# Which matmuls of a seven-product step run ahead of the next step's first: a change of order on TensorE

## The chip, the cores and the metric

One core of one Trainium2 chip. The metric is the device time of one execution in microseconds (us): the median of three runs before the change, and the same for the changed kernel. A profile is one execution of its own, with its own time. The engines are called as the profile calls them: PE (TensorE's matmuls), PEld (TensorE's weight loads), DVE (VectorE), ACT (ScalarE), POOL (GpSimd), SP (SyncE).

## What is computed

A decoder trunk of two layers on 256 positions of width 2048, all in float32. What matters here are its five matrix products per layer, the last above all:

```python
for l in range(DEPTH):                      # 2 layers
    h = rms_norm(x, norm1_g[l])
    z = h @ w_in[l]                         # 2048 x 5120
    ...                                     # attention and gated groups give mix
    x = x + mix @ w_out[l]                  # 2048 x 2048
    h2 = rms_norm(x, norm2_g[l])
    x = x + jnp.square(jax.nn.relu(h2 @ w_up[l])) @ w_down[l]   # 2048 x 8192, 8192 x 2048
return rms_norm(x, final_g)
```

## The kernel before

**Numbers.** Every weight and every activation is split in two parts, a rounded high part and the low rest. A product of two such numbers is made of three matmuls: high by high, low by high, high by low. The weights come from memory in blocks of 128 x 1024 (`Sub`), which SP's queue loads into one of 7 raw buffers; ACT makes the high part (`high`, line 167) and DVE the low part (`low`, line 177). There are 6 buffers each for high and for low parts.

**Steps.** The work of TensorE is a list of steps in a fixed order, and everything else hangs on it. Before a step is issued, the high and low parts of some sub-blocks ahead are issued (lines 1004 and following), and delayed work (`soon`, `later`) whose time has come. Time is counted in sub-blocks done. There are three kinds of steps that carry weights:

- Channel-major steps (`transposed`, matmuls at lines 400, 402 and 404): one sub-block, two blocks of 128 output channels (`cb`) by four blocks of rows (`k`) by three matmuls, 24 in all. The weights stand in the array, 256 positions of the activation stream through it. The first matmul of a step needs its high part, the second (line 402) its low part.
- Position-major steps (`natural`, lines 459 to 461), 12 matmuls of 512 columns. They do not stand near the change.
- Seven-product steps (`fast`, matmuls at lines 430, 432 and 433), for a part of the columns of `w_down`. They make a 2 x 2 block product from seven products instead of eight, by sums and differences of blocks (Winograd's form of Strassen's scheme). Here the activations stand in the array and 256 columns of weights stream. One step has four sub-blocks: two that are loaded (`Top`, `Bottom`) and two made of sums (`Sums`), for which DVE runs four subtractions (lines 218, 219, 222 and 223). The sub-blocks are used in the order top, bottom, first sums (`upper`), second sums (`lower`). Each of the seven products is two blocks `k` by three matmuls, so a step has 42.

**Where a seven-product step ends.** Six of the products, 36 matmuls, are issued in the step. The seventh, which uses `lower` as the sixth does, is put into the list `left_over`, and the next channel-major step issues its 6 matmuls behind its own first three (line 395). Each seven-product step is followed by a channel-major step.

**Where the results go.** Two steps (`p` 0 and 1) make one group. The first six results of a group lie in halves of three banks of the accumulator memory, the seventh in a half of a bank of its own. When the group's second step is done, ACT copies the three banks (line 901) for groups 1 and 2, and the seventh half five sub-blocks later (line 887; for group 0 line 869). GpSimd adds the copies up in memory over the eight row blocks of `w_down` (line 866).

**Where the steps stand.** In each layer the up and down projections run in nine rounds `e`. Round `e` makes 1024 hidden channels from `w_up` and uses those of round `e - 1` with `w_down`. `ORDER` and `USUAL` give the place of each seven-product step among the channel-major ones, for instance ahead of steps 2 and 3, 7 and 9, 13 and 14. At the end of the up projection of a round DVE has more to do: it makes low parts of the new hidden channels (line 643) and sums of them (lines 796 to 799), and the seven-product steps that follow need those.

Of the kernel before, what the change touches and what calls it, by code (L numbers as in the profile page):

```python
# [35 lines left out]
P = 128  # L36
# [29 lines left out]
USUAL = ((7, 9), (2, 3), (13, 14))  # L66
WARM = 11
HALVES = 5
D_SCORES, D_NORM, D_TURN, D_VALUES = 2, 1, 3, 2


# [19 lines left out]
def trunk(ctx: ExitStack, tc: tile.TileContext, layout, xT, consts, gains, w, b_sp, w_sp, out):  # L91
# [11 lines left out]
    vec, act, pe = nc.vector, nc.scalar, nc.tensor  # L103
# [30 lines left out]
    def acc_bank(i=None, of=4):  # L134

        if i is None:
            i = bank_at[0] = (bank_at[0] + 1) % of
        return pacc.tile([P, 512], F32, name=f"acc{i}", tag=f"acc{i}")
# [61 lines left out]
    class Bottom(Sub):  # L200


        left, right, frees = Top.left, Top.right, 0
# [46 lines left out]
    def run_due(calls=due):  # L250
        for item in [i for i in calls if i[0] <= now[0]]:
            calls.remove(item)
            item[1]()
# [102 lines left out]
    left_over = []  # L356
    summed, sum_parts = [True], [None]

    def sums_ready():
        run_until(lambda: summed[0])  # L360
# [8 lines left out]
    def transposed(name, l, row0, nk, col0, ncols, moving, after, between=None, apart=False, of=4, cols=None):  # L369

        cols = cols or range(0, ncols, 256)
        order = [(c, k) for c in cols for k in range(0, nk, 4)]
        if between:
            h = nk // 8
            order[h:2 * h], order[2 * h:3 * h] = order[2 * h:3 * h], order[h:2 * h]  # L380
        accs = {}
        for n, (c, k0) in enumerate(order):
            if between and n == nk // 4:
                mark(between)
            wt = Sub(name, l, row0 + k0 * P, col0 + c, 4, 256)

            def mm(wt=wt, k0=k0, c=c):
                two = apart and c == cols[-1]
                if k0 == 0:
                    accs[c] = [acc_bank(of=of), acc_bank(of=of)] if two else acc_bank(of=of)  # L390
                ps = accs[c]
                for cb in range(2):
                    o = ps[cb][:, 0:S] if two else ps[:, cb * S:(cb + 1) * S]
                    for k in range(4):
                        if cb == 0 and k == 1 and left_over:
                            left_over.pop()()
                        xs = moving(k0 + k)
                        hi = wt.hi[:, k, cb * P:(cb + 1) * P]
                        last = k0 + k == nk - 1
                        pe.matmul(o, lhsT=hi, rhs=xs[:, 0, :], start=(k0 + k == 0 and (two or cb == 0)), stop=False,  # L400
                                  skip_group_check=True)
                        pe.matmul(o, lhsT=wt.lo[:, k, cb * P:(cb + 1) * P], rhs=xs[:, 0, :], start=False, stop=False,  # L402
                                  skip_group_check=True)
                        pe.matmul(o, lhsT=hi, rhs=xs[:, 1, :], start=False, stop=last, skip_group_check=True)  # L404
            steps.append((wt, mm, (lambda c=c: after(c, accs[c])) if k0 + 4 == nk else None))

    def fast(name, l, row0, col0, tiles, slots, fresh, last, done):

        o = []
        for p in range(2):
            top, bottom = (cls(name, l, row0 + (4 * h + 2 * p) * P, col0, 2, 512) for h, cls in enumerate((Top, Bottom)))
            upper, lower = Sums(top, bottom, False), Sums(top, bottom, True)

            def mm(p=p, top=top, bottom=bottom, upper=upper, lower=lower):
                if p == 0:
                    o.extend(slots())  # L420
                half = tiles[0][0]
                sums_ready()
                extra = sum_parts[0]
                left, right = slice(0, 256), slice(256, 512)

                def product(n, a, lower_rows, tt, b, cols):
                    for k in range(2):
                        xh, xl = (a[:, 4 * lower_rows + 2 * p + k, i, tt * P:(tt + 1) * P] for i in range(2))
                        hi, lo = b.hi[:, k, cols], b.lo[:, k, cols]
                        pe.matmul(o[n], lhsT=xh, rhs=hi, start=(p == 0 and k == 0 and n in fresh), stop=False,  # L430
                                  skip_group_check=True)
                        pe.matmul(o[n], lhsT=xh, rhs=lo, start=False, stop=False, skip_group_check=True)  # L432
                        pe.matmul(o[n], lhsT=xl, rhs=hi, start=False, stop=(n in last and p == 1 and k == 1),  # L433
                                  skip_group_check=True)

                for n, args in enumerate((
                        (half, 0, 0, top, left), (half, 1, 0, bottom, left), (extra, 1, 0, bottom, right),
                        (extra, 1, 1, upper, left), (extra, 0, 1, upper, right), (extra, 0, 0, lower, right))):
                    product(n, *args)
                left_over.append(lambda: product(6, half, 1, 1, lower, left))  # L440
            steps.append(((top, bottom, upper, lower), mm, (lambda: done(o)) if p and done else None))

    def natural(name, l, col0, ncols, after):
# [20 lines left out]
    def mark(fn):  # L464

        steps.append((None, fn, None))
# [484 lines left out]
    def load_more():  # L951
        while n_load[0] < len(subs):
# [6 lines left out]
            if 0 < c < KC:  # L959
                nc.sync.dma_start(x[:, c:c + 2, :], xv[:, c:c + 2, :])  # L960
            subs[n_load[0]].load(2 if n_load[0] < HALVES else 1)
            n_load[0] += 1
            n_raw[0] += 1

    def high_to(n, parts=1):
        while n_high[0] < min(n, len(subs)):
            if not subs[n_high[0]].loads:
                low_to(n_high[0] - subs[n_high[0]].second)
            subs[n_high[0]].high(parts)
            n_high[0] += 1  # L970

    def low_to(n, parts=1):
        while n_low[0] < min(n, len(subs)):
            subs[n_low[0]].low(parts)
            n_raw[0] -= subs[n_low[0]].frees
            n_low[0] += 1
# [22 lines left out]
    for n, (wt, mm, after) in enumerate(steps):  # L999
# [3 lines left out]
        else:  # L1003
            ahead = min(2 + max(done - 10, 0) // 2, LO_BUFS - 2)
            if done + 2 < KC // 2:
                norms[0].chunks(2 * done + 4)
            high_to(min(done + 2 + ahead, HALVES), 2)
            high_to(done + 2 + ahead)
            run_due()
            low_to(min(done + 1 + ahead, HALVES), 2)  # L1010
            low_to(done + 1 + ahead)
# [12 lines left out]
    n = norms[-1]  # L1024
# [43 lines left out]
```

## Time and profile before

| What | Value |
|---|---|
| Median of 3 runs | 2031.38 us (2031.15 to 2032.34) |
| Profiled execution, its own time | 2032.32 us |
| Its span, first to last instruction | 2030.5 us |
| Mean granted TensorE clock | 0.997 |
| Matmuls | 16834 |
| Data read and written in device memory | 394.58 MB and 22.02 MB |

The profiled execution's time is 1.8 us longer than its span. A busy matmul in the profile is not a matmul at its peak: each is shown with about 0.28 us, and they overlap, since they start a good 0.11 us apart. So the busy share says little, and the starts in the timeline say how fast TensorE really goes. A weight load (PEld) runs beside the matmul before it. A "releaser" behind an arrow names what an instruction waited for.

### The profile page before, as it was taken

How to read it: one execution, taken by the hardware profiler on the slowest of the kernel's cores; microseconds unless marked ns; L12 is line 12 of the kernel's file. 1: busy time of each engine (PE TensorE's matmuls, PEld its weight loads, DVE VectorE, ACT ScalarE, POOL GpSimd, SP SyncE). 2: the span in 40 equal slices, each digit the busy share in tenths (PEclk: the TensorE clock that was granted, in tenths of full speed). 3: DMA queues.
4: the chain of work that ended last, by engine and by line, in shares of the span. 5: the costliest groups of instructions: out<-in, count | busy, mean ns of one | idle time of the engine just before them, and what ended most of it. 6: DMA issues, size and time to landing. Idle time of an engine off the chain costs nothing.

```text
span 2030.5 us, 40718 instructions
## 1 busy us (share of the span) xinstructions
PE 2017.7 (99%) x16834; PEld 1979.0 (97%) x16834; DVE 1577.2 (78%) x1950; ACT 1213.3 (60%) x1613; POOL 157.1 (8%) x200
## 2 busy tenths in 40 slices
PE   9999999999999999999999999999999999999997
PEld 8998999999999999999989989999999999999997
DVE  7566766688888898898856667667888898888985
ACT  7565454566566666765645654556666666667654
POOL 0002300000001000100000032000000000010000
PEclk9999999999999999999999999999999999999998
DMA  9555556567678776865664555565676777777562
GB/s 326 193 168 166 187 187 202 173 229 210 214 221 238 237 227 197 246 220 202 207 213 161 167 187 187 188 199 184 212 227 210 226 234 217 237 215 256 186 217 88
DMA packets 126443, 419.27 MB, mean 206 GB/s; under 512 B 14128, under 2 KB 22064, under 8 KB 126256
## 3 DMA queue, kind: packets, MB, share of 16 engines
q1 hardware_dynamic: 110800, 389.86, 57.3%
q0 software_dynamic: 14304, 23.86, 6.9%
q8 instruction: 132, 2.16, 0.4%
q10 hardware_dynamic: 1152, 2.94, 0.4%
q14 instruction: 55, 0.45, 0.1%
HBM read 394.58 MB, written 22.02 MB: 205 GB/s over the span
## 4 chain that ended last, share of the span: by engine, by line
PE 95%; DVE 3%; ACT 1%; issue 1%; DMA 1%; ACTq 0%; DVEq 0%; SPq 0%
PE acc L402 23%; PE acc L400 23%; PE acc L404 23%; PE acc L461 3%; PE acc L459 3%; PE acc L460 3%; PE aux L430 3%; PE aux L432 3%; PE acc L432 3%; PE aux L433 3%; PE acc L433 3%; PE acc L430 3%; DVE lo L177 1%; ACT hi L167 0%; PE aux L693 0%
## 5 line engine op out<-in xcount | busy, mean ns | idle before, releaser
L167 ACT ACTIVATE hi<-raw 128x1024 fp32r<-128x1024 f32 (+1 forms) x817 | 836.1, 1051 | 495.5 <-DVE raw L219 231.0
L177 DVE TENSOR_TENSOR lo<-raw,hi 128x1024 fp32r<-128x1024 f32 (+1 forms) x817 | 964.1, 1213 | 155.3 <-ACT hi L167 152.0
L400 PE MATMUL acc<-hs,hi 128*128 128x256 f32 x2816 | 781.2, 277 | 0.0
L402 PE MATMUL acc<-hs,lo 128*128 128x256 f32 x2816 | 779.3, 277 | 0.2
L404 PE MATMUL acc<-hs,hi 128*128 128x256 f32 x2816 | 778.2, 276 | 0.0
L402 PEld LDWEIGHTS acc<-hs,lo 128*128 128x128 f32 x2816 | 528.8, 188 | 2.5 <-DVE lo L177 1.8
L400 PEld LDWEIGHTS acc<-hs,hi 128*128 128x128 f32 x2816 | 528.8, 188 | 0.4 <-issue 0.2
L404 PEld LDWEIGHTS acc<-hs,hi 128*128 128x128 f32 x2816 | 528.7, 188 | 0.0
L400 PE MATMUL acc<-half,hi 128*128 128x256 f32 x1344 | 371.9, 277 | 0.0
L402 PE MATMUL acc<-half,lo 128*128 128x256 f32 x1344 | 371.0, 276 | 0.0
L404 PE MATMUL acc<-half,hi 128*128 128x256 f32 x1344 | 371.0, 276 | 0.0
L402 PEld LDWEIGHTS acc<-half,lo 128*128 128x128 f32 x1344 | 252.3, 188 | 0.0
L400 PEld LDWEIGHTS acc<-half,hi 128*128 128x128 f32 x1344 | 252.3, 188 | 0.0
L404 PEld LDWEIGHTS acc<-half,hi 128*128 128x128 f32 x1344 | 252.3, 188 | 0.0
L866 POOL DMA_DIRECT2D far<-ar x92 | 74.7, 983 | 1159.2 <-ACT ar L869 606.3
L432 PE MATMUL acc<-lo,shared 128*128 128x256 f32 x384 | 106.5, 277 | 0.0
L433 PE MATMUL acc<-hi,shared 128*128 128x256 f32 x384 | 106.1, 276 | 0.0
L430 PE MATMUL acc<-hi,shared 128*128 128x256 f32 x384 | 106.0, 276 | 0.0
L459 PE MATMUL acc<-hi,hs 128*128 128x512 f32 x256 | 101.6, 397 | 0.0
L461 PE MATMUL acc<-hi,hs 128*128 128x512 f32 x256 | 100.7, 393 | 0.0
L460 PE MATMUL acc<-lo,hs 128*128 128x512 f32 x256 | 99.9, 390 | 0.5 <-DVE lo L177 0.5
L643 DVE TENSOR_TENSOR half<-ar,half 128x512 fp32r<-128x512 f32 x72 | 49.7, 690 | 62.2 <-ACT half L640 61.2
(163 smaller groups left out, 2560.9 us busy)
## 6 DMA issues: line engine op xcount, KB each, us to landing
raw<-in_w SPq DMA_DIRECT2D x731, 512.0 KB, 4.6
far<-ar POOLq DMA_DIRECT2D x60, 256.0 KB, 6.8
far<-ar POOLq DMA_DIRECT2D x32, 128.0 KB, 4.4
ar<-far POOLq DMA_DIRECT2D x12, 256.0 KB, 9.0
raw<-in_w SPq DMA_DIRECT2D x10, 256.0 KB, 5.2
x<-in_xT SPq DMA_DIRECT2D x7, 256.0 KB, 5.6
out<-x SPq DMA_DIRECT2D x7, 256.0 KB, 3.1
shared<-in_b_sp ACTq DMA_DIRECT2D x2, 512.0 KB, 8.0
```

The costliest lines, as they stand in the source:

```text
L167: act.activation(self.h[:, j * m:(j + 1) * m], self.raw[:, j * m:(j + 1) * m], AF.Copy)
L177: vec.tensor_tensor(lo[:, r], self.raw[:, r], self.h[:, r].bitcast(F32), op=OP.subtract)
L400: pe.matmul(o, lhsT=hi, rhs=xs[:, 0, :], start=(k0 + k == 0 and (two or cb == 0)), stop=False, skip_group_check=True)
L402: pe.matmul(o, lhsT=wt.lo[:, k, cb * P:(cb + 1) * P], rhs=xs[:, 0, :], start=False, stop=False, skip_group_check=True)
L404: pe.matmul(o, lhsT=hi, rhs=xs[:, 1, :], start=False, stop=last, skip_group_check=True)
L430: pe.matmul(o[n], lhsT=xh, rhs=hi, start=(p == 0 and k == 0 and n in fresh), stop=False, skip_group_check=True)
L432: pe.matmul(o[n], lhsT=xh, rhs=lo, start=False, stop=False, skip_group_check=True)
L433: pe.matmul(o[n], lhsT=xl, rhs=hi, start=False, stop=(n in last and p == 1 and k == 1), skip_group_check=True)
L459: pe.matmul(ps, lhsT=xh, rhs=hi, start=(k0 + k == 0), stop=False)
L460: pe.matmul(ps, lhsT=xh, rhs=lo, start=False, stop=False)
L461: pe.matmul(ps, lhsT=xl, rhs=hi, start=False, stop=(k0 + k == KC - 1))
L866: nc.gpsimd.dma_start(far[g][:, r], src, **({} if e == max(g, 1) else {"accum_op": OP.add}))
```

## The change

The three matmuls of a product are no longer issued in place but collected as calls. All 42 of a seven-product step are collected in the old order; all but the last `BEHIND` = 1 are issued in the step, and the last one goes to `left_over`. The channel-major step issues what is left over ahead of its matmul number `BETWEEN` = 1 of each first column block, that is behind its first matmul instead of behind its first three. So where the order was 36 matmuls, 3 of the next step, 6, and then the rest of the next step, it is now 41, 1 of the next step, 1, and the rest. The matmuls themselves, their operands and the flags that begin and end a sum are those of before.

```diff
--- before.py
+++ after.py
@@ -66,6 +66,7 @@
 USUAL = ((7, 9), (2, 3), (13, 14))
 WARM = 11
 HALVES = 5
+BEHIND, BETWEEN = 1, 1
 D_SCORES, D_NORM, D_TURN, D_VALUES = 2, 1, 3, 2
 
 
@@ -392,16 +393,16 @@
                 for cb in range(2):
                     o = ps[cb][:, 0:S] if two else ps[:, cb * S:(cb + 1) * S]
                     for k in range(4):
-                        if cb == 0 and k == 1 and left_over:
-                            left_over.pop()()
                         xs = moving(k0 + k)
-                        hi = wt.hi[:, k, cb * P:(cb + 1) * P]
-                        last = k0 + k == nk - 1
-                        pe.matmul(o, lhsT=hi, rhs=xs[:, 0, :], start=(k0 + k == 0 and (two or cb == 0)), stop=False,
-                                  skip_group_check=True)
-                        pe.matmul(o, lhsT=wt.lo[:, k, cb * P:(cb + 1) * P], rhs=xs[:, 0, :], start=False, stop=False,
-                                  skip_group_check=True)
-                        pe.matmul(o, lhsT=hi, rhs=xs[:, 1, :], start=False, stop=last, skip_group_check=True)
+                        hi, lo = (t[:, k, cb * P:(cb + 1) * P] for t in (wt.hi, wt.lo))
+                        first, last = k0 + k == 0 and (two or cb == 0), k0 + k == nk - 1
+                        for j, (lhs, rhs) in enumerate(((hi, 0), (lo, 0), (hi, 1))):
+                            if left_over and 3 * k + j == BETWEEN:
+                                for call in left_over:
+                                    call()
+                                left_over.clear()
+                            pe.matmul(o, lhsT=lhs, rhs=xs[:, rhs, :], start=(first and j == 0), stop=(last and j == 2),
+                                      skip_group_check=True)
             steps.append((wt, mm, (lambda c=c: after(c, accs[c])) if k0 + 4 == nk else None))
 
     def fast(name, l, row0, col0, tiles, slots, fresh, last, done):
@@ -423,21 +424,25 @@
                 extra = sum_parts[0]
                 left, right = slice(0, 256), slice(256, 512)
 
+                calls = []
+
                 def product(n, a, lower_rows, tt, b, cols):
                     for k in range(2):
                         xh, xl = (a[:, 4 * lower_rows + 2 * p + k, i, tt * P:(tt + 1) * P] for i in range(2))
                         hi, lo = b.hi[:, k, cols], b.lo[:, k, cols]
-                        pe.matmul(o[n], lhsT=xh, rhs=hi, start=(p == 0 and k == 0 and n in fresh), stop=False,
-                                  skip_group_check=True)
-                        pe.matmul(o[n], lhsT=xh, rhs=lo, start=False, stop=False, skip_group_check=True)
-                        pe.matmul(o[n], lhsT=xl, rhs=hi, start=False, stop=(n in last and p == 1 and k == 1),
-                                  skip_group_check=True)
+                        for j, (lhs, rhs) in enumerate(((xh, hi), (xh, lo), (xl, hi))):
+                            calls.append(lambda k=k, j=j, lhs=lhs, rhs=rhs: pe.matmul(
+                                o[n], lhsT=lhs, rhs=rhs, start=(p == 0 and k == 0 and j == 0 and n in fresh),
+                                stop=(n in last and p == 1 and k == 1 and j == 2), skip_group_check=True))
 
                 for n, args in enumerate((
                         (half, 0, 0, top, left), (half, 1, 0, bottom, left), (extra, 1, 0, bottom, right),
-                        (extra, 1, 1, upper, left), (extra, 0, 1, upper, right), (extra, 0, 0, lower, right))):
+                        (extra, 1, 1, upper, left), (extra, 0, 1, upper, right), (extra, 0, 0, lower, right),
+                        (half, 1, 1, lower, left))):
                     product(n, *args)
-                left_over.append(lambda: product(6, half, 1, 1, lower, left))
+                for call in calls[:-BEHIND]:
+                    call()
+                left_over.extend(calls[-BEHIND:])
             steps.append(((top, bottom, upper, lower), mm, (lambda: done(o)) if p and done else None))
 
     def natural(name, l, col0, ncols, after):
```

## The prediction

> **What bounds the kernel now.** I read the page first, then the tensor engine's timeline around the steps that the change touches, then the waits, then VectorE beside the boundaries that wait.
>
> ```profile
> span 2030.5 us, 40718 instructions
> ...
> PE 2017.7 (99%) x16834; PEld 1979.0 (97%) x16834; DVE 1577.2 (78%) x1950; ACT 1213.3 (60%) x1613; POOL 157.1 (8%) x200
> ...
> PE 95%; DVE 3%; ACT 1%; issue 1%; DMA 1%; ACTq 0%; DVEq 0%; SPq 0%
> ```
>
> The matmuls (PE) are busy for 99% of the span, and 95% of the chain that ended last runs over them. No matmul is added or removed (before and after a seven-product step issues 42), so the only thing that can change is the spacing of the matmuls: either they wait, or they follow each other more slowly than elsewhere. A busy share of 99% cannot show either, because a matmul of 0.28 us overlaps the next; what counts is the distance from one start to the next.
>
> Below is the timeline of the tensor engine around one seven-product step (starts in the first column, us). L430 to L433 are matmuls of the step, L400 to L404 those of channel-major steps.
>
> ```profile
> 398.05 0.28 PE L430 MATMUL aux<-hi,shared 128*128 128x256 f32 x1
> ...
> 400.77 0.28 PE L400 MATMUL acc<-hs,hi 128*128 128x256 f32 x1
> ...
> 401.12 0.28 PE L430 MATMUL aux<-hi,half 128*128 128x256 f32 x1
> ...
> 401.83 0.28 PE L400 MATMUL acc<-hs,hi 128*128 128x256 f32 x1
> ...
> 402.19 0.28 PE L400 MATMUL acc<-hs,hi 128*128 128x256 f32 x1
> ```
>
> The step's last 24 matmuls before the boundary start from 398.05 on, and the next step's first at 400.77: 2.72 us over 24, or 113.3 ns apart. That is the undisturbed pace. Then come three matmuls of the channel-major step, the six left over, and the channel-major step again. From 400.77 to 402.19 there are 12 distances in 1.42 us, 118.3 ns each; at 113.3 they would take 1.36. So this mixed piece loses about 0.06 us (the rows round to 0.01): 0.01 in its first three distances (0.35), 0.03 in the six of the product (0.71), 0.02 in the three after (0.36). Nothing waits there; the matmuls only follow each other more slowly.
>
> How many such boundaries there are, a group of VectorE tells that each step runs once, the last of the four subtractions that make its sums:
>
> ```profile
> L223 DVE TENSOR_TENSOR raw<-raw 128x512 f32<-128x512 f32 x76 | 52.7, 693 | 2.6
> ```
>
> 76 steps, 38 in each layer.
>
> Some boundaries also wait. The row is from the list of waits (us in total, times, longest); below it stand timeline rows of four places.
>
> ```profile
> PEld acc L402 <- DVE lo L177: 1.8, 8, 0.3
> ```
>
> ```profile
> 802.29 0.28 PE L400 MATMUL acc<-hs,hi 128*128 128x256 f32 x1
> 802.58 0.38 PE L402 MATMUL acc<-hs,lo 128*128 128x256 f32 x1
> 802.80 0.28 PE L404 MATMUL acc<-hs,hi 128*128 128x256 f32 x1
> ...
> 810.34 0.28 PE L400 MATMUL acc<-hs,hi 128*128 128x256 f32 x1
> 810.67 0.38 PE L402 MATMUL acc<-hs,lo 128*128 128x256 f32 x1
> 810.89 0.28 PE L404 MATMUL acc<-hs,hi 128*128 128x256 f32 x1
> ...
> 924.38 0.28 PE L400 MATMUL acc<-hs,hi 128*128 128x256 f32 x1
> 924.60 0.39 PE L402 MATMUL acc<-hs,lo 128*128 128x256 f32 x1
> 924.82 0.28 PE L404 MATMUL acc<-hs,hi 128*128 128x256 f32 x1
> ...
> 1929.35 0.28 PE L400 MATMUL acc<-hs,hi 128*128 128x256 f32 x1
> 1929.56 0.38 PE L402 MATMUL acc<-hs,lo 128*128 128x256 f32 x1
> 1929.78 0.28 PE L404 MATMUL acc<-hs,hi 128*128 128x256 f32 x1
> ```
>
> The second matmul of the next step (L402) needs that step's low part, which VectorE makes at L177, and eight times its weight load sits idle for it: four per layer, at 802 and 810 and, one row block later, at 887 and 895. At 924 and its twin at 1929 the same matmul is late by less than that list shows. Two distances at 810 take 0.55 us where two at the 0.118 of the mixed piece take 0.235: 0.31 lost (0.22 of the second distance is the weight load, no longer hidden). At 802 it is 0.51, so 0.28 lost; at 924 0.44, 0.20 lost; at 1929 0.43, the same. Ten boundaries of 76 wait.
>
> **The change part by part.** Five of the six left-over matmuls move ahead of the next step's first matmul; the sixth comes after it, ahead of the L402 that waits. Order before: 36 F, T T T, 6 F, T ...; after: 41 F, T, 1 F, T T .... (F of the seven-product step, T of the next.) No DMA is issued by a moved matmul, and no queue of SP, ACT or POOL is passed. No wait is added: the seventh product reads the second sums tile, which the sixth product has just read, and writes a bank half whose last reader (the ACT copies at L869 and L887) runs at least five sub-blocks after the step before. The six copied bank halves are complete after the same 36 matmuls, so ACT's L901 starts when it did. The sums tile is let go two or three matmuls earlier, 0.2 to 0.3 us, which can only help ACT and VectorE. I take all this at nothing; if the early release did matter, it would be a gain.
>
> First term, the waits. The L402 of the next step came 37 matmuls after the step's first and now comes 43 after it: 6 x 0.113 = 0.68 us later, against a lateness of at most 0.31. So it waits nowhere any more, if VectorE keeps its times. What is late next? At 802 the step that follows, one channel-major step on, waits too, for the low part of its first sums tile:
>
> ```profile
> 798.43:808.18 9.75, 9.74 (x85) 9.49 (x83) 9.64 (x12) 4.73 (x7) 0.00 (x0) 1.00 0.48 163
> 808.33:811.75 3.42, 3.37 (x28) 3.17 (x28) 3.42 (x3) 3.00 (x5) 0.00 (x0) 1.00 0.74 207
> ```
>
> ```profile
> 808.06 0.28 PE L430 MATMUL acc<-hi,shared 128*128 128x256 f32 x1
> ...
> 808.46 0.28 PE L433 MATMUL acc<-hi,shared 128*128 128x256 f32 x1
> ```
>
> Two distances in 0.40 us, 0.17 lost inside the step. In the two rows above (a stretch, its length, and the busy us of PE, PEld, DVE, ACT, POOL in it) VectorE works 9.64 of 9.75 us and then 3.42 of 3.42. It has no slack there, so the low part for 808.23 comes when it came, and a tensor engine that arrives 0.3 us earlier waits 0.3 us longer: what 802 gains, 808 takes back. The same holds at 887. After 808 the tensor engine starts from the same instant as before; the L402 of 810 finds its low part at the same time but asks for it 0.68 us later, so those 0.31 us stay. Gain: 4 x 0.31 (810, 895 and their twins) + 2 x 0.20 (924, 1929) = 1.64 us.
>
> Second term, the mixed piece. After the change it holds one F and about four T instead of six F and five or six T. I let the cost go with the number of matmuls: of the 0.06, the product's 0.03 falls to that of one matmul (0.005 to 0.01) and the opening three distances to one (0.01 to under 0.005), while the 0.02 behind the last F stays. That leaves 0.03, a gain of 0.03 at each boundary. The trace has no row with one F between T, so the bounds are: nothing gained (the cost is that of the three changes of kind, which remain), 0.06 gained (one matmul disturbs nothing), and a loss, worked out below. I take 0.03, from the rows nearest in kind. The 66 boundaries without a wait give 66 x 0.03 = 2.0, the six above 6 x 0.03 = 0.2, the other four nothing, as 808 sets the time.
>
> Against this stands a rule. The Trainium skill ("TensorE: Matmul & The Clock Gate", Part 2, "Step-by-step" and "Back-to-back issue gap") has the weight load pulled ahead of matmuls in flight into a background buffer, and the distance of matmuls in a row set by their columns alone, which by its formula is an estimated 109 ns at 256 columns, whatever stood before. The trace does not agree at the mixed piece (118.3 ns against 113.3, same columns, no wait). By the rule the mixed piece would cost nothing and only the waits would be gained.
>
> Sum: 1.64 + 2.2 = 3.8 us. The profiled execution took 2032.3 us (span 2030.5 and 1.8 around it), 0.9 over the median of the three timed runs; 2032.3 - 3.8 = 2028.5 there, and 2031.4 - 3.8 = 2027.6 for the median.
>
> **The rivals.** *The mixed piece gives nothing.* Its cost belongs to the three changes between F and T, which remain, and only the waits go: 1.64 us, 2029.7. For it speaks that the last three distances, behind the change, cost as much each as any; against it that the six F cost half of the whole. What the rule above predicts comes to the same time.
>
> *The whole mixed cost goes.* One F is too short to upset the pace: 66 x 0.06 + 4 x 0.37 + 2 x 0.26 = 6.0 us, 2025.4. Against it: the first distances are slow before any F has come back.
>
> *Nothing is given back at 808.* If VectorE's stretch is really driven by the tensor engine, 802 and 887 and their twins add 4 x 0.31 = 1.2: 5.0 us, 2026.3. The full rows of VectorE speak against it.
>
> *Slower: the slow pace is not left.* At one boundary it was not:
>
> ```profile
> 925.64 0.28 PE L400 MATMUL acc<-hs,hi 128*128 128x256 f32 x1
> ...
> 930.94 0.27 PE L839 MATMUL acc<-con,ar 128*128 128x128 f32 x1
> ```
>
> Behind the left-over product at 924, 45 channel-major matmuls took 5.30 us, 117.8 ns each, until other work came in; at 401.83 three sufficed. Six F in a row may be what brings the pace back, and one F may not be enough. If every boundary were followed by 45 such matmuls, it would cost 45 x 4.5 ns = 0.20 each, 15 us over 76: 2031.4 - 1.6 + 15 = 2045. It decides as soon as the slow piece lasts some 5 matmuls longer than the 11 or 12 of today (5 x 4.5 ns x 76 = 1.7 us eats the first term). Against it: it happened once in the two layers, at a boundary that had waited, and its twin at 1929 was left as usual.
>
> *The change does nothing.* Were the waits shifted rather than removed and the mixed piece as slow, 2031.4.
>
> **How the numbers follow.** A difference of 0.2%, 4.1 us, is about what a measurement of this kernel can tell from no change. Forecast 0.50, its own range 3.0 to 4.8 us of gain by the rounding of the 0.03 and the local pace; 0.20 of that lies beyond 4.1 us. The whole cost gone 0.12; nothing given back 0.08; only the waits 0.17; nothing 0.03; slower 0.10. Faster by over 0.2%: 0.20 + 0.12 + 0.08 = 0.40. Within: 0.30 + 0.17 + 0.03 = 0.50. Slower: 0.10. The range reaches from the second rival, 2025.4, over the first, 2029.7, and somewhat above it for the spread of the runs, to 2030.9; outside lie the slower case, most of no change and a little else.
>
> **What would show it.** In the profile after: the weight load of the next step's first low part no longer waits for L177 at the ten boundaries, or only in traces of it; the stop at 808 grows from 0.17 to about 0.45; from the next step's first matmul on, the pace is back to 113.3 within five distances instead of twelve; the span is near 2026.7. Wrong would be: a slow pace that lasts through the channel-major steps, mixed pieces that lose 0.06 as before, or a gain at 802 that shows at the end.

## The result, and the profile after

The changed kernel is slower: 2038.99 us (2038.85 to 2039.72 in 6 runs) against 2031.88 us (2031.15 to 2035.74 in 6 runs) of the kernel before in the same comparison, a ratio of 1.0034 with a 95% interval of 1.0024 to 1.0044. Its profiled execution took 2039.43 us, 7.1 us more than that of before, and the difference lies in the span:

```profile
span 2037.7 us, 40718 instructions
...
PE 2025.5 (99%) x16834; PEld 1988.7 (98%) x16834; DVE 1576.9 (77%) x1950; ACT 1213.8 (60%) x1613; POOL 157.9 (8%) x200
```

The same matmuls, the same 99%, and 7.2 us more. VectorE and ScalarE have the same instructions and, to 0.5 us, the same busy time as before. So either TensorE waits more or its matmuls follow each other more slowly. First the waits, from the list of waits of the weight loads (us in total, times, longest). In the changed kernel all matmuls of a channel-major step have line 404 and all of a seven-product step line 434:

```profile
PEld acc L434 <- DVE lo L178: 0.9, 4, 0.2
...
PEld acc L404 <- issue: 0.5, 2, 0.2
```

Of the eight waits that the list showed at the head of channel-major steps none is left. The list now shows four inside the seven-product steps, at the places that were at 808 and 893 before and at their twins in the second layer. They took over what was gained ahead of them. The timeline shows the first (from here on "x2" in a row means that two matmuls are merged in it):

```profile
810.87 0.39 PE L434 MATMUL acc<-hi,shared 128*128 128x256 f32 x2
811.30 0.39 PE L434 MATMUL acc<-lo,shared 128*128 128x256 f32 x1
811.53 0.40 PE L434 MATMUL acc<-hi,shared 128*128 128x256 f32 x2
```

From the second matmul of the first row (a little under 0.12 after 810.87) to 811.53 two distances take 0.54 us, 0.31 more than two at 0.113; it was 0.17 before. The waits have gone as predicted, so the time went into the distances. Here are the first boundary of the changed kernel and the second:

```profile
400.87 0.28 PE L404 MATMUL acc<-hs,hi 128*128 128x256 f32 x1
400.99 0.28 PE L434 MATMUL aux<-hi,half 128*128 128x256 f32 x1
401.10 0.28 PE L404 MATMUL acc<-hs,lo 128*128 128x256 f32 x1
...
409.47 0.28 PE L434 MATMUL aux<-hi,half 128*128 128x256 f32 x1
...
414.30 0.28 PE L404 MATMUL acc<-hs,hi 128*128 128x256 f32 x1
414.42 0.28 PE L434 MATMUL aux<-hi,half 128*128 128x256 f32 x1
414.54 0.29 PE L404 MATMUL acc<-hs,lo 128*128 128x256 f32 x1
414.66 0.40 PE L404 MATMUL acc<-hs,hi 128*128 128x256 f32 x2
...
422.60 0.28 PE L434 MATMUL acc<-hi,half 128*128 128x256 f32 x1
```

The order is the new one: one L404, one L434, then L404 on. From 401.10 to the next seven-product step at 409.47 there are 71 distances (the rest of this step and two whole ones): 8.37 us, 117.9 ns each. The seven-product step itself, 41 distances to 414.30, takes 4.83 us, 117.8 each. Nothing waits in either. Behind the second boundary, from 414.66 to 422.60, 70 distances take 7.94 us, 113.4 each. So the slow pace that the prediction saw for only twelve distances at this boundary lasts from the first boundary to the second, through three channel-major steps and a whole seven-product step, and is left there. The third boundary sets it off again. In the kernel before, the stretch behind the first boundary was fast: from the row at 402.19 in the prediction to the next seven-product step there are 66 distances in 7.48 us, 113.3 each.

```profile
409.67 0.28 PE L430 MATMUL aux<-hi,half 128*128 128x256 f32 x1
```

Neither the clock nor the traffic beside the matmuls tells the two paces apart. The rows below show the three stretches of the changed kernel, slow, slow and fast: a stretch, its length, the busy us of PE, PEld, DVE, ACT and POOL, the granted clock, the busy share of the DMA engines and the GB/s that they moved. The clock is 1.00 in all three, the third stretch has at least as much DMA traffic as the first, and the share of its time that VectorE is busy (81%) lies between those of the first two (91% and 68%).

```profile
401.10:409.47 8.37, 8.37 (x74) 8.37 (x73) 7.58 (x9) 4.71 (x6) 0.00 (x0) 1.00 0.47 154
409.47:414.30 4.83, 4.83 (x44) 4.83 (x42) 3.29 (x5) 3.70 (x4) 0.00 (x0) 1.00 0.94 249
414.66:422.60 7.94, 7.94 (x72) 7.94 (x71) 6.46 (x8) 4.85 (x7) 0.78 (x1) 1.00 0.50 180
```

Counted from the starts of all matmuls of these two kinds of steps in the nine rounds of both layers (a distance of 115.5 to 135 ns as slow, a longer one as a stop):

```
              slow distances  over 113.3 ns, in all   stops, over 113.3 ns, in all
before              913              4.7 us                  4.3 us
after              3228             14.9 us                  1.8 us
```

So 10.2 us were lost to the pace and 2.5 gained at stops: 7.7, against 7.2 in the span.

### The profile page after: what moved, and what is told of

It is laid out like the page before. It is cut to its first block, busy times and chain, and to the rows that moved or that the text cites. A ratio compares the mean times of both kernels' runs of the same rounds, so it can differ in the third digit from the quotient of the medians.

```text
span 2037.7 us, 40718 instructions
## 1 busy us (share of the span) xinstructions
PE 2025.5 (99%) x16834; PEld 1988.7 (98%) x16834; DVE 1576.9 (77%) x1950; ACT 1213.8 (60%) x1613; POOL 157.9 (8%) x200
## 4 chain that ended last, share of the span: by engine, by line
PE 99%; DVE 0%; ACT 0%; issue 0%; DVEq 0%
PE acc L404 70%; PE acc L434 10%; PE aux L434 8%; PE acc L466 3%; PE acc L464 3%; PE acc L465 3%; PE aux L698 0%; PE aux L634 0%; PE aux L592 0%; PE aux L621 0%; PE aux L991 0%; DVE x L1035 0%; PE aux L595 0%; PE aux L636 0%; PE acc L844 0%; PE aux L533 0%
## 5 line engine op out<-in xcount | busy, mean ns | idle before, releaser
L404 PE MATMUL acc<-hs,hi 128*128 128x256 f32 x5632 | 991.7, 278 | 0.0
L404 PEld LDWEIGHTS acc<-hs,hi 128*128 128x128 f32 x5632 | 859.5, 188 | 0.4 <-issue 0.2
L404 PE MATMUL acc<-hs,lo 128*128 128x256 f32 x2816 | 780.5, 277 | 0.0
L404 PEld LDWEIGHTS acc<-hs,lo 128*128 128x128 f32 x2816 | 530.8, 188 | 0.4 <-issue 0.2
L404 PE MATMUL acc<-half,hi 128*128 128x256 f32 x2688 | 461.9, 276 | 0.0
L404 PEld LDWEIGHTS acc<-half,hi 128*128 128x128 f32 x2688 | 406.4, 188 | 0.0
L404 PE MATMUL acc<-half,lo 128*128 128x256 f32 x1344 | 371.0, 276 | 0.0
L404 PEld LDWEIGHTS acc<-half,lo 128*128 128x128 f32 x1344 | 252.3, 188 | 0.0
L434 PE MATMUL acc<-hi,shared 128*128 128x256 f32 x768 | 140.9, 278 | 0.0
L434 PEld LDWEIGHTS acc<-hi,shared 128*128 128x128 f32 x768 | 119.9, 188 | 0.0
L434 PE MATMUL aux<-hi,half 128*128 128x256 f32 x528 | 112.1, 278 | 0.0
L434 PE MATMUL acc<-lo,shared 128*128 128x256 f32 x384 | 107.0, 279 | 0.1
L434 PEld LDWEIGHTS aux<-hi,half 128*128 128x128 f32 x528 | 87.6, 188 | 0.0
L434 PE MATMUL aux<-hi,shared 128*128 128x256 f32 x448 | 82.2, 278 | 0.0
L504 DVE TENSOR_TENSOR x<-x,acc 128x512 f32<-128x512 f32 (+1 forms) x49 | 33.0, 674 | 57.6 <-PE acc L404 57.3
```

The lines of the kernel that those rows point to most:

```text
L404: pe.matmul(o, lhsT=lhs, rhs=xs[:, rhs, :], start=(first and j == 0), stop=(last and j == 2), skip_group_check=True)
L434: calls.append(lambda k=k, j=j, lhs=lhs, rhs=rhs: pe.matmul(o[n], lhsT=lhs, rhs=rhs, start=(p == 0 and k == 0 and j == 0 and n in fresh), ...
L504: vec.tensor_tensor(xj, xj, ps[j][:, 0:S] if alone else pair(ps)[:, j, :], op=OP.add)
```

## The experiments

F is again a matmul of the seven-product step, T one of the channel-major step. A pair such as 1, 3 gives `BEHIND` and `BETWEEN`. All but two of the kernels change only these two numbers; in all of them the two slices that use `BEHIND` are written so that zero works too:

```diff
-BEHIND, BETWEEN = 1, 1
+BEHIND, BETWEEN = 1, 3
...
-                for call in calls[:-BEHIND]:
+                for call in calls[:len(calls) - BEHIND]:
...
-                left_over.extend(calls[-BEHIND:])
+                left_over.extend(calls[len(calls) - BEHIND:])
```

The theory after the result was that each full return from F to T (to at least two T in a row) turns the pace over, from fast to slow or back. Before the change there are two returns at each boundary (ahead of the three T, and behind the six F), so the pace ends where it began. With one T alone between two F there is only one full return, so each boundary turns it. The first rival was the prediction's own reason: six F in a row bring the pace back and one does not. The second: the slow pace is set off where an F is issued between the first and the second matmul of the next step (the split).

**One behind three** (`BEHIND, BETWEEN = 1, 3`).

> 41 matmuls of the seven-product step, three of the next step, the last one, the rest. Theory (turning): each return from the seven-product step to at least two matmuls in a row of the channel-major step turns the pace over, from 113.3 to 117.6 ns or back; here there are two such returns per boundary, so every boundary ends at 113.3. The second matmul of the next step still comes 5 matmuls later than before, so the waits for its low part are gone: about 2028 us, 3 to 4 below the kernel before. Rival (six matmuls): six matmuls of a product in a row bring the pace back and one does not: about 2039 as the changed kernel, the slow pace behind every other boundary. Second rival (split): the slow pace is set off by issuing a foreign matmul between the first and the second of the next step: here it is not, 2028.

2034.3 us (2032.6 to 2037.1 in 10 runs), ratio 1.0011 [1.0002, 1.0020]. The first rival falls: one F brought the pace back at all 60 boundaries that began fast. But the time misses the 2028 of the theory. In the profiled execution 16 boundaries began slow and ended slow. They begin with the stop inside the seven-product step: behind it the step goes on at the slow pace, two returns leave that pace as they leave the fast one, and it lasts over several boundaries. The profiled execution, at 2037.1 us, was the longest of the ten; how many such boundaries the others had, no profile shows.

**One behind two** (`1, 2`).

> 41 matmuls, two of the next step, the last one, the rest. Theory (turning): two matmuls in a row are enough for a turn, so two turns per boundary, pace back to 113.3 within about six distances: about 2028 us. If three in a row are needed, one turn: about 2039. Rival (six matmuls): about 2039. Rival (split): 2028.

2028.94 us (2028.5 to 2029.7 in 10 runs), ratio 0.9984 [0.9974, 0.9993]: faster than both kernels, as the theory said, and as the second rival said too. Its timeline at the first boundary:

```profile
401.40 0.28 PE L404 MATMUL acc<-hs,hi 128*128 128x256 f32 x1
401.52 0.28 PE L404 MATMUL acc<-hs,lo 128*128 128x256 f32 x1
401.64 0.28 PE L434 MATMUL aux<-hi,half 128*128 128x256 f32 x1
401.76 0.40 PE L404 MATMUL acc<-hs,hi 128*128 128x256 f32 x2
...
409.72 0.28 PE L434 MATMUL aux<-hi,half 128*128 128x256 f32 x1
```

From 401.76 to 409.72 there are 70 distances in 7.96 us, 113.7 each, with a few longer distances at the start. All 76 boundaries end fast, also the two that a stop had made slow, which the theory did not say: by it they should have stayed slow. The low part of the next step is asked for 0.57 us later than before (five matmuls), and the waits for it are gone, as in the changed kernel.

**Six behind one** (`6, 1`).

> 36 matmuls, one of the next step, the whole seventh product, the rest. Theory (turning): one matmul alone turns nothing, so there is one turn per boundary, and the slow pace stands behind every other boundary, about 2039 us. Rival (six matmuls): the six in a row bring the pace back, about 2028. Rival (split): 2039, since the product stands between the first and the second matmul.

2040.66 us, ratio 1.0040 [1.0025, 1.0055]. The first rival falls a second time: six F in a row do not bring the pace back behind a single T.

```profile
400.46 0.28 PE L404 MATMUL acc<-hs,hi 128*128 128x256 f32 x1
...
401.28 0.28 PE L404 MATMUL acc<-hs,lo 128*128 128x256 f32 x1
...
409.64 0.28 PE L434 MATMUL aux<-hi,half 128*128 128x256 f32 x1
```

The product stands between the first two rows; from 401.28 to 409.64 71 distances take 8.36 us, 117.7 each.

**None behind** (`0, 1`).

> All 42 matmuls in the step, none behind. Theory (turning): one return, one turn per boundary: the slow pace lasts from one boundary to the next and is left there, about 2038 to 2039 us. Rival (six matmuls): nothing brings the pace back, so it is slow from the first boundary on until other work comes, 2045 or more. Rival (split): nothing is split and nothing mixed, all at 113.3: about 2026.

2038.81 us, ratio 1.0033 [1.0020, 1.0046], as the theory said, and against both rivals: nothing is split here, and the pace is left at every other boundary with no F behind.

```profile
401.19 0.28 PE L404 MATMUL acc<-hs,hi 128*128 128x256 f32 x1
...
409.68 0.28 PE L434 MATMUL aux<-hi,half 128*128 128x256 f32 x1
...
414.63 0.28 PE L404 MATMUL acc<-hs,hi 128*128 128x256 f32 x1
...
422.80 0.28 PE L434 MATMUL acc<-hi,half 128*128 128x256 f32 x1
```

72 distances to 409.68 take 8.49 us (117.9), 42 to 414.63 take 4.95 (117.9), 72 to 422.80 take 8.17 (113.5).

Fast and slow alternate here as the two steps of a group do, so the place in the group could be the cause as well. The changed kernel tells the two apart. Of its 38 first steps of a group 36 turned the pace to slow. The other two, the last groups of the layers, came slow, since the stop inside the step before them had shifted the order, and they turned it to fast. The turn goes with the pace that arrives, not with the place.

**Six behind two** (`6, 2`), to have the waits by themselves.

> 36 matmuls, two of the next step, the whole seventh product, the rest. The second matmul of the next step stands where it stood before, so the ten waits for its low part come back; there are two full returns per boundary as in the version with one behind two. Theory (turning, and the waits apart from it): pace back to 113.3 behind each boundary, the waits as before, so about 1.5 to 2 us over the version with one behind two, 2030.5 to 2032. Rival (the waits cost nothing in the end): as that version, 2029.

2032.18 us, ratio 1.0001 [0.9992, 1.0011], at the upper end of what was expected, and the waits are back:

```profile
PEld acc L404 <- DVE lo L178: 1.9, 8, 0.3
```

Against one behind two it is 3.2 us more, also 3.2 by the spans (2030.7 and 2027.5). By the count of distances, 1.8 of that are stops and 1.5 are slow distances (a longer mixed piece, and two boundaries that began slow and stayed so).

**Two behind two** (`2, 2`).

> 40 matmuls, two of the next step, two behind, the rest. Theory (turning): two returns, pace back, waits gone; the slow piece is about as long as with one behind two: 2028 to 2029.5. If two matmuls of the product behind are another disturbance than one, the place where the pace comes back moves, and a turn may be missed: 2039.

2063.07 us, ratio 1.0154 [1.0137, 1.0171]. That is a miss of every case written down. The first boundary turns the pace to slow, and none brings it back:

```profile
401.41 0.28 PE L404 MATMUL acc<-hs,hi 128*128 128x256 f32 x1
401.53 0.28 PE L404 MATMUL acc<-hs,lo 128*128 128x256 f32 x1
401.65 0.28 PE L434 MATMUL aux<-lo,half 128*128 128x256 f32 x1
401.77 0.28 PE L434 MATMUL aux<-hi,half 128*128 128x256 f32 x1
401.88 0.40 PE L404 MATMUL acc<-hs,hi 128*128 128x256 f32 x2
...
410.13 0.28 PE L434 MATMUL aux<-hi,half 128*128 128x256 f32 x1
```

70 distances from 401.88 take 8.25 us, 117.9 each. At 74 of the 76 boundaries the pace ends slow, whichever it was: with two F between, the count of returns doesn't tell.

**What stands and what streams.** Two kernels asked which operand's change turns the pace. Both begin from "none behind", change the operands of the seventh product alone and so compute another result. Each ran once. The first has streaming activations, the second standing weights:

```diff
-                        hi, lo = b.hi[:, k, cols], b.lo[:, k, cols]
+                        hi, lo = (hs[:, 4 * lower_rows + 2 * p + k, i, :] for i in range(2)) if n == 6 else (b.hi[:, k, cols], b.lo[:, k, cols])
```

> None behind, and the seventh product streams activations (of the hidden state's normalised input) through the array in place of weights, so that its result is another number; its standing operand stays the activations. Theory (turning, by the standing operand): the pace turns where the weights come to stand in the array again, at the next step's first matmuls, 42 behind the step's first. Theory (turning, by the streaming operand): it turns where activations stream again, behind the 36th. Rival (the next step's first weight loads, which carry waits, set it off): behind the 42nd.

```diff
+                        xh, xl = (b.hi[:, k, 0:P], b.lo[:, k, 0:P]) if n == 6 else (xh, xl)
```

> None behind, and the seventh product has weights standing in the array in place of activations, so that its result is another number; weights stream through it as in the other six. By the standing operand: the pace turns behind the 36th matmul of the step. By the streaming operand: behind the 42nd. Rival (the next step's first weight loads with their waits): behind the 42nd.

With streaming activations the run took 2065.64 us, with standing weights 2029.73. The timelines around the seventh product, first of the one with streaming activations, then of the one with standing weights:

```profile
400.96 0.88 PE L434 MATMUL aux<-hs,half 128*128 128x256 f32 x6
401.68 0.28 PE L404 MATMUL acc<-hs,hi 128*128 128x256 f32 x1
...
410.16 0.28 PE L434 MATMUL aux<-hi,half 128*128 128x256 f32 x1
```

```profile
400.64 0.28 PE L435 MATMUL aux<-hi 128*128 128x256 f32 x1
...
401.36 0.29 PE L404 MATMUL acc<-hs,hi 128*128 128x256 f32 x1
...
401.61 0.39 PE L404 MATMUL acc<-hs,hi 128*128 128x256 f32 x2
...
409.54 0.28 PE L435 MATMUL aux<-hi,half 128*128 128x256 f32 x1
```

In both the six distances of the seventh product take 0.72 us, 120 ns each, so the pace turns behind the 36th matmul, inside the step. The list of waits has no weight load that waits there, so a turn does not need one: the rival of the waiting weight loads falls. Behind it they part. With streaming activations the pace stays slow (72 distances to 410.16 in 8.48 us, 117.8), and 70 of the 76 boundaries began slow and ended slow, where one turn at each would alternate. With standing weights it turns back at the next step (70 from 401.61 to 409.54 in 7.93 us, 113.3), and all 76 boundaries end fast. Neither the standing nor the streaming operand alone decides: the pace turned when the stream alone went from weights to activations, and when the standing operand alone went from activations to weights. In the second kernel the seventh product also takes both operands from the same two buffers; no run separates that.

Not every change turns it. From T to F, where both operands change, the pace stayed as it was at all 76 beginnings of a seven-product step, in all 14 profiles. Inside a step the standing activations change from one buffer to another (`half` to `shared`, at 398.05 in the prediction's rows), and the pace stays at 113.3.

**How many F behind.** Three kernels asked what was wrong with two: `2, 3`, then `3, 3`, then `3, 2`.

> 40 matmuls, three of the next step, two behind, the rest. With two behind two, which took 2063, either the two matmuls in a row of the seven-product step were too few, or the two of the next step ahead of them. Theory (turning, a return needs enough matmuls of the next step): three ahead make a full return, the pace comes back, 2029 to 2034 as one behind three. Rival (two in a row of the product cannot turn the pace back): slow throughout, near 2063.

> 39 matmuls, three of the next step, three behind, the rest: whole groups of three on both sides, as before the change, but three behind in place of six. Theory (turning): fast behind nearly every boundary, 2028 to 2034. Rival (six are needed): slow behind boundaries, 2039 or more.

> 39 matmuls, two of the next step, three behind, the rest. Theory (two of the next step ahead are enough with one or six behind, and two behind was the exception): 2028 to 2030. Rival (with two ahead only some lengths end fast): slow behind the boundaries, 2039 to 2063.

They took 2064.14 us (1.0160 [1.0131, 1.0190]), 2035.85 (1.0016 [1.0005, 1.0027]) and 2032.38 (1.0002 [0.9990, 1.0013]). So two behind is slow with two as with three ahead. Three behind kept the fast pace at all 60 boundaries that began fast, and kept the slow one at all 16 that began slow. Both kernels with three behind took longer than expected (2034 and 2030 at most), though less than their rivals said. The last run asked whether it is the length of two or the place in the group of three at which the left-over piece begins:

> 37 matmuls, two of the next step, five behind, the rest. Two behind ended slow whatever stood ahead; one, three and six behind ended fast. Theory (only the length of two is special): fast behind the boundaries, 2029 to 2033. Rival (where in its group of three the left-over piece begins): two behind and five behind both begin with the second matmul of a group, so five also ends slow, near 2063.

2032.21 us, ratio 0.9995 [0.9984, 1.0007]: 70 of the 76 boundaries end fast. So the place in the group of three is not the reason. Of the lengths tried behind two or three T, only two ends slow; four was not tried. (The kernel before had a median of 2033.84 in this comparison, against 2031.7 to 2032.0 in the others.)

All orders beside each other, with the pace in the step's 30th to 36th matmul and in the later part of the next step (slow: over 116 ns), counted over the 76 boundaries of each profile ("fast-slow" began fast and ended slow):

```
                     fast-fast  fast-slow  slow-fast  slow-slow   median us
before (6, 3)            71         1          4          0        2031.9
after (1, 1)              0        40         36          0        2039.0
none behind               0        39         37          0        2038.8
6, 1                      0        38         36          2        2040.7
1, 2                     74         0          2          0        2028.9
1, 3                     60         0          0         16        2034.3
6, 2                     70         0          4          2        2032.2
5, 2                     67         2          3          4        2032.2
3, 2                     60         0          0         16        2032.4
3, 3                     60         0          0         16        2035.9
2, 2                      0         6          2         68        2063.1
2, 3                      0         4          0         72        2064.1
streaming activations     0         5          1         70        2065.6
standing weights         72         0          4          0        2029.7
```

The profiled execution of 3, 2 took 2035.1 us, the longest of its 8, so its 16 slow boundaries need not stand in the median run. The last two rows are one run each.

## Why the prediction was wrong

*The waits: right.* The L404 that asks for the low part waits at none of the ten boundaries. The 1.64 us were the right size: where the pace comes back (one behind two), stops fell from 4.3 to 2.6 us.

*The gain at 802 is taken back at 808: right.* The stop there grew from 0.17 to 0.31 us in the changed kernel, less than the 0.45 expected; TensorE came there at the slow pace, so later. With one behind two it came at the fast pace and lost what was expected: the four stops inside steps are 0.44 to 0.47 us there, against 0.29 to 0.32 here.

*The mixed piece: wrong, and here the prediction failed.* The step was "I let the cost go with the number of matmuls", taken from one kind of boundary, at which the slow pace always ended. It took the 0.06 us for a price of mixing. It is the price of a pace that is set off at one return and ended at the next; with the second return taken away, the pace lasted to the next boundary. 0.03 us less at 66 boundaries was forecast; 40 boundaries instead began a slow stretch, and 2315 more distances of about 4.4 ns over the fast pace cost 10.2 us. "A slow pace that lasts through the channel-major steps" was among the prediction's own signs of being wrong.

*The slower rival had the place but not the reason.* It priced a pace that is not left, 45 matmuls behind every boundary, at 15 us, and decided by six F against one. The runs showed one F to suffice behind two or three T, and six not to suffice behind one. Between the kernel before and the changed one, what decided was `BETWEEN`, not `BEHIND` (which decides at two behind). The row that it had (45 matmuls at 117.8 ns behind the boundary at 924) showed that the pace can last; the chance of 0.10 gave it too little weight, and the range left it out.

*The rule that the columns alone set the distance.* The section that the prediction took its formula from (the Trainium skill, "TensorE: Matmul & The Clock Gate", "Back-to-back issue gap") gives it for an isolated matmul, says that in a stream of load and matmul pairs both set the spacing, and has no second pace. Here the same 256 columns, each with its own weight load, ran at 113.3 or at 117.8 ns for whole steps without a wait, so the columns alone do not set the distance.

Open stays why. That the count of full returns decides holds for the three orders with one or no T ahead (but for two boundaries of 6, 1), and for the boundaries that begin fast, all but three, in the orders with two or three T ahead and one, three, five or six F behind. It does not tell why two F behind nearly always end slow, nor why one behind two (at two boundaries) and the kernel before (at four) end fast from the slow pace too, while 6, 2 and 5, 2 do both. Standing and streaming operands both turn the pace; what in the array or its reads differs between the two paces no profile here shows.

## What to carry to other kernels

Where TensorE is busy throughout, look at the distance between matmul starts, not at their busy time: two paces 4% apart can hide under the same 99%. Before making a short disturbance shorter, ask what ends it, and count from the trace in which pace the stream goes on behind each boundary; here the piece that looked like a cost was also the way back. An order with two such paces is tried in several variants and judged by that count, since a neighbouring one (two behind instead of one) was 34 us worse.

## What the runs showed of the hardware

The pace of a stream of 256-column matmuls, each with its own weight load, has two values that hold for hundreds of matmuls without any wait, 113.3 and 117.8 ns, at a granted clock of 0.997 to 0.998 in all runs. It turned on the way from F to T, and inside a step where the stream alone went from weights to activations or the standing operand alone from activations to weights. It never turned on the way from T to F. It also turned behind some stops: to slow behind all four stops inside steps in the kernel before and behind two of four with one behind two, to fast behind two of four in the changed kernel. Two kernels that differ in one moved matmul per boundary (1, 2 and 2, 2) lie 1.7% apart.
